# One core, two decoder layers: the convolution's taps, the last rows of the output projection and the prefetch depths are set anew

## The chip, the cores and the metric

The kernel runs on one core of a Trainium2 chip. The time is device microseconds of one launch. A core has TensorE (PE, matmuls), VectorE (DVE), ScalarE (ACT), GpSimd (POOL, hardly used here) and SyncE (SP, which issues the DMAs). Each works through its own queue of instructions in the order in which they stand; between queues there are only semaphores.

## The reference

Two layers on 256 tokens of 1024 features, in float32. A layer is a SwiGLU feed-forward part, a mixer, and a second feed-forward part; each reads an RMS norm of x and adds to x. The mixer is what the change touches:

```python
h = rms_norm(x, mix_norm[l])
p = h @ w_in[l]                                     # 19 tiles of 128 columns
a_val, a_gate, b_u, b_v, c_b, c_c, c_x = split(p)
a = a_val * sigmoid(a_gate)                         # group A: 384 channels
a = causal_depthwise_conv(a, conv_a_w[l]) + conv_a_b[l]      # 31 taps
a = silu(layer_norm(a, ln_a_g[l], ln_a_b[l]))
b = chunked_spatial_gating(gelu(b_u), gelu(b_v), ...)        # group B: 256 channels, a layer norm over v
c = c_b * causal_depthwise_conv(c_c * c_x, conv_c_w[l])      # group C: 384 channels, 3 taps
x = x + concatenate([a, b, c]) @ w_out[l]           # 8 blocks of 128 rows
```

## The kernel before, in words

**Weights.** All weights are one stream of pages of 128x1024 floats, in the order of their use. SyncE loads a page into one of RAWS buffers (`load_to`), ScalarE rounds it to a high part (`hi`, L157), and VectorE subtracts that from the page (`lo`, L158). The pairs lie in a pool of 30 buffers (`parts`, tag "pg"), which also holds the work tiles of the convolution. With a pair, a product of float32 numbers is three matmuls of the reduced type: high by high, high by low, low by high (`mm_three` L204 to L206, `mm_out` L216 to L218). `native` hands out the raw page instead, and `mm_out` then makes one float32 matmul (L212), which the trace shows as two records. `split_to` splits ahead of use as far as `state["cap"]` allows, `load_to` loads LOAD_AHEAD pages further.

**Mixer.** Layout is channels on partitions, tokens along the row. `proj` makes one of the 19 tiles of the combined projection, 24 matmuls of 128x256 each, 456 in all; their order is A (gate and value, three times), B's v and u, then for each of C's three tiles C_C, C_X, C_B. After each tile `drain(BACK)` issues four pieces of group A's convolution. `conv_ops` cuts the 31 taps of one 128-channel tile in two kinds: WIDE of them are products on ScalarE (L591, L594), four at a time into a 128x1024 tile, and VectorE adds each further four to the sum (L596); the rest are multiply-and-adds of 128x256 on VectorE (L603). L605 and L606 fold the four partial sums into the tile `m_ac`.

**Group B.** The layer norm over v takes a matmul for the mean (L565), squares, a matmul for the sum of squares (`m_lv_ps`, L336), the reciprocal root on VectorE as eleven small operations (L303 to L317, the last gives `m_lv_out`), and a broadcast on TensorE (`m_lv_pb`, L326). VectorE reads that (L723), then come transposes (`m_pt`, L732), copies, the gating matmuls (`m_pz`, L743), L749 and L756.

**Group C.** L690 to L703: `m_cc`, `zpad`, three taps, `m_cr`, and L703, which multiplies the C_B tile out of PSUM into the result (`m_co` or `m_cv`: buffers are used again, and names change). With the third tile only the three MM buffers of PSUM are left for projections (`use([MM], [SM])`), so the third C_B tile takes the buffer of the second, which L703 frees.

**Output projection (L764 on).** Rows of `w_out` come in OUT_ORDER (5, 6, 3, 4, 7, then group A's 0, 1, 2), four banks each. Between these matmuls stand the steps of group A's layer norm (`m_la`), after the matmuls whose counts CHAIN names. Then y (L781), Silu (L783), and the three rows of group A from native pages. `drain_banks` then finishes bank by bank, with the next norm's transposes (L393) between.

**Order.** Matmuls of the output projection and the sums are pinned to the order of the program; those of `proj` and everything on the other engines are put in order by the framework's scheduler, which works from costs of its own.

Of the kernel before, what the change touches and what calls it, by code (L numbers as in the profile page):

```python
# [20 lines left out]
DT = D // P  # L21
# [3 lines left out]
NA, NB, NC = 3, 2, 3  # L25
# [30 lines left out]
OUT_ORDER = (5, 6, 3, 4, 7, 0, 1, 2)  # L56

PAGE = 1024
RAWS = 6
PARTS = 15  # L60
LOAD_AHEAD = 6
AHEAD = 11
PACE = 1.6
NEXT = 4
WORK = 10
EVAC = 6
WARM = 8
LAG = 4
OPEN = 3
LAST = 3  # L70
CHAIN = (7, 11, 15)
STEPS = 3
AFTER = 2
WIDE = 16
BACK = 4


# [1 line left out]
def hybrid_trunk(ctx, tc, x_t, x_n, par, gain, w_st, b_s, wts, out):  # L79
    nc = tc.nc  # L80
    const = ctx.enter_context(tc.tile_pool(name="const", bufs=1))
    raws = ctx.enter_context(tc.tile_pool(name="raws", bufs=RAWS))
    parts = ctx.enter_context(tc.tile_pool(name="parts", bufs=2 * PARTS))
    acts = ctx.enter_context(tc.tile_pool(name="acts", bufs=1))
    work = ctx.enter_context(tc.tile_pool(name="work", bufs=WORK))
    tmp = ctx.enter_context(tc.tile_pool(name="tmp", bufs=2))
# [16 lines left out]
    banks = [(c, h) for h in range(2) for c in range(TC)]  # L103
    state = {"at": 0, "cap": None, "credit": 0.0, "mm": [], "sm": []}
# [3 lines left out]
    def use(mm, sm):  # L108

        state["mm"], state["sm"], state["outs"] = list(mm), list(sm), 0  # L110
# [14 lines left out]
    pages = []  # L125
# [3 lines left out]
    def after(ins, first):  # L129

        if first is not None:
            tc.add_manual_dep(
                ins.ins, first.ins.name,
                mybir.DependencyInfo(mybir.DependencyClass.NoSync, mybir.DependencyReason.DATA),
                reason="order",
            )
# [3 lines left out]
    def load_to(n):  # L140
        while len(loaded) < min(n, n_pages):
            i = len(loaded)
            raw = raws.tile([P, PAGE], F32, tag="raw", name=f"raw{i}")
            nc.sync.dma_start(raw, wts[i])
            loaded.append(raw)

    def split_to(n):

        while len(pages) < min(n, n_pages if state["cap"] is None else state["cap"]):
            i = len(pages)  # L150
            load_to(i + LOAD_AHEAD)
            hi = parts.tile([P, PAGE], F32R, tag="pg", name=f"hi{i}")
            lo = parts.tile([P, PAGE], F32R, tag="pg", name=f"lo{i}")
            step = PAGE if i > 3 else N
            for o in range(0, PAGE, step):
                cut = slice(o, o + step)
                nc.scalar.copy(hi[:, cut], loaded[i][:, cut])  # L157
                after(nc.vector.tensor_sub(lo[:, cut], loaded[i][:, cut], hi[:, cut]), held[0])  # L158
            pages.append((hi, lo))

    def native(n):

        at = state["at"]
        state["at"] += n
        load_to(at + n - 1 + LOAD_AHEAD)
        while len(pages) < at + n:
            pages.append(None)
        return loaded[at:at + n]

    def weights(n, ahead=True):  # L170

        at = state["at"]
        state["at"] += n
        last = at + n
        split_to(last)
        if ahead:
            state["credit"] += n * PACE
            to = min(last + AHEAD, len(pages) + int(state["credit"]))
            state["credit"] -= max(0, to - len(pages))
            state["credit"] = min(state["credit"], 2.0)  # L180
            split_to(to)
        return pages[at:at + n]
# [396 lines left out]
    def conv_ops(l, i, ap, out, name):  # L579
# [17 lines left out]

        single = list(range(WIDE, WA))
        groups = WIDE // 4
        for n in range(groups):  # L600
# [7 lines left out]
    def mixer(l, norm, nxt):  # L608
# [8 lines left out]
        use([MM, MM, MM, DD[0], DD[1]], [SM, DD[2], DD[3]])  # L617
        state["cap"] = state["at"] + NIN + OPEN

# [32 lines left out]
        def split_mix(k):  # L652
            if not halves:
                pair = parts.tile([P, 2, 2, T], F32R, tag="pg", name=f"{nm}_mix{k}")
                halves.extend([pair[:, 1], pair[:, 0]])
            x2 = halves.pop()
            nc.scalar.copy(x2[:, 0, :], mix[k])
            nc.vector.tensor_sub(x2[:, 1, :], mix[k], x2[:, 0, :])
            mix[k] = x2
# [106 lines left out]
        po = {b: ps_d.tile([P, N], F32, tag=f"d{b[0]}{b[1]}", name=f"{nm}_po{b[0]}{b[1]}")  # L766
              for b in banks}
        first, last = OUT_ORDER[0], OUT_ORDER[-1]
        state["cap"] = state["at"] + NB + NC
        ws = weights(NB + NC, False)  # L770
        ln = layer_norm(conv, LN_EPS, f"{nm}_la")
        got = None
        for n, k in enumerate(OUT_ORDER[:DT - NA]):
            for i, (c, h) in enumerate(banks):
                mm_out(po[c, h], mix[k], ws[n], c, h, k == first, k == last)
                if n * len(banks) + i in CHAIN:
                    got = next(ln)
        xc, pr = got
        for i in range(NA):
            y = single(f"{nm}_ay{i}")  # L780
# [1 line left out]
            a = single(f"{nm}_ao{i}")  # L782
            nc.scalar.activation(a, y, AF.Silu, scale=col(l, "ln_a_g", i), bias=col(l, "ln_a_b", i))  # L783
            mix[i] = a
        wn = dict(zip(OUT_ORDER[DT - NA:], native(NA)))
        state["cap"] = None
        split_to(state["at"] + NEXT)

# [88 lines left out]
```

## Time and profile before

| | us |
|---|---|
| median of 3 runs | 944.25 |
| lowest, highest | 943.35, 946.89 |
| profiled execution, time | 945.05 |
| profiled execution, span of the trace | 943.3 |
| PE busy in the span | 930.4 |
| DVE busy | 697.7 |
| ACT busy | 531.9 |

The span is cut by stages: feed-forward parts at 20 to 184, 292 to 464, 480 to 650 and 758 to 930 us, mixers at about 184 to 292 and 650 to 758 us. The trace's matmul records overlap: the length of one record is longer than the distance to the next, and the distance is what a matmul costs in a row of them. Where "x8" stands in a timeline row, eight equal instructions are drawn together, and the length is that of all. "[0.70 <-DVE m_co L703]" says that the engine sat idle for 0.70 us before and that VectorE's instruction of line 703 released it.

### The profile page before, as it was taken

Reading aid. Unit: us, or ns where it says so; the run is one execution under the profiler, and the core shown is the slowest. Engines: PE = TensorE matmul, PEld = TensorE weight load, DVE = VectorE, ACT = ScalarE, POOL = GpSimd, SP = SyncE. Lnnn points to the kernel's source line nnn. Section 1 sums busy time; section 2 is a strip of 40 time slices with the busy share of each in tenths; the row PEclk is TensorE's granted clock in tenths of the full one; section 3 lists DMA queues with packets and bytes.
Section 4 is the critical chain, followed back from the end, with each engine's and each line's share of the span. In section 5 each row is a group of like instructions: output and inputs, shape, how many; then the busy total and the mean of one; then the engine's idle time right before and its main releaser. Section 6 shows DMA issues by size and latency. Waiting matters only on the chain.

```text
span 943.3 us, 13962 instructions
## 1 busy us (share of the span) xinstructions
PE 930.4 (99%) x5192; PEld 799.7 (85%) x5192; DVE 697.7 (74%) x1195; ACT 531.9 (56%) x905; POOL 3.5 (0%) x14
## 2 busy tenths in 40 slices
PE   9999999999999999999999999999999999999996
PEld 8888888899868888888888888888998688888885
DVE  6996666589979976666697666666899798666624
ACT  5775454467457755545465545454755586555512
POOL 0000000000000000000000000000000000000000
PEclk9999999999999999999999999999999999999999
DMA  8897555524047955555465555553430588555201
GB/s 305 310 348 260 183 190 190 178 81 166 4 149 259 341 196 186 191 189 186 149 212 191 190 188 185 194 182 133 135 112 1 201 303 300 194 189 196 91 1 44
DMA packets 49459, 172.22 MB, mean 183 GB/s; under 512 B 5616, under 2 KB 7024, under 8 KB 49392
## 3 DMA queue, kind: packets, MB, share of 16 engines
q1 hardware_dynamic: 49392, 171.34, 51.6%
q8 instruction: 40, 0.66, 0.3%
q14 instruction: 27, 0.22, 0.1%
HBM read 170.27 MB, written 1.05 MB: 182 GB/s over the span
## 4 chain that ended last, share of the span: by engine, by line
PE 86%; DVE 9%; ACT 2%; issue 2%; DMA 1%; SPq 0%; DVEq 0%; ACTq 0%
PE f_pu L197 17%; PE f_pg L197 17%; PE f_pu L198 9%; PE f_pg L198 9%; PE f_pd L216 8%; PE f_pd L217 8%; PE f_pd L218 8%; DVE m_ac_acc L603 3%; DVE lo L158 2%; PE m_po L212 2%; DVE m_ac_acc L596 2%; PE m_p L204 1%; PE m_p L205 1%; PE m_p L206 1%; PE m_po L216 1%
## 5 line engine op out<-in xcount | busy, mean ns | idle before, releaser
L158 DVE TENSOR_TENSOR lo<-raw,hi 128x1024 fp32r<-128x1024 f32 (+1 forms) x310 | 376.0, 1218 | 166.1 <-ACT hi L157 147.0
L157 ACT CAST hi<-raw 128x1024 fp32r<-128x1024 f32 (+1 forms) x310 | 321.7, 1047 | 231.9 <-PE f_pu L197 79.6
L197 PE MATMUL f_pu<-ffn_norm_x,hi 128*128 128x512 f32 x696 | 250.1, 399 | 0.0
L197 PE MATMUL f_pg<-ffn_norm_x,hi 128*128 128x512 f32 x688 | 246.5, 398 | 0.0
L198 PE MATMUL f_pu<-ffn_norm_x,lo 128*128 128x256 f32 x696 | 195.2, 280 | 0.0
L198 PE MATMUL f_pg<-ffn_norm_x,lo 128*128 128x256 f32 x688 | 192.8, 280 | 0.0
L197 PEld LDWEIGHTS f_pu<-ffn_norm_x,hi 128*128 128x128 f32 x696 | 130.7, 188 | 31.9
L197 PEld LDWEIGHTS f_pg<-ffn_norm_x,hi 128*128 128x128 f32 x688 | 129.2, 188 | 31.0 <-issue 0.5
L216 PE MATMUL f_pd<-hi,f_m 128*128 128x512 f32 x352 | 138.7, 394 | 0.0
L217 PE MATMUL f_pd<-lo,f_m 128*128 128x512 f32 x352 | 137.8, 392 | 0.0
L218 PE MATMUL f_pd<-hi,f_m 128*128 128x512 f32 x352 | 137.2, 390 | 0.0
L198 PEld LDWEIGHTS f_pg<-ffn_norm_x,lo 128*128 128x128 f32 x688 | 129.7, 189 | 3.2 <-issue 0.5
L198 PEld LDWEIGHTS f_pu<-ffn_norm_x,lo 128*128 128x128 f32 x696 | 131.5, 189 | 0.1
L204 PE MATMUL m_p<-mix_norm_x,hi 128*128 128x256 f32 x304 | 87.2, 287 | 1.4 <-DVE m_co L703 0.7
L206 PE MATMUL m_p<-mix_norm_x,lo 128*128 128x256 f32 x304 | 86.0, 283 | 0.0
L205 PE MATMUL m_p<-mix_norm_x,hi 128*128 128x256 f32 x304 | 86.0, 283 | 0.0
L216 PEld LDWEIGHTS f_pd<-hi,f_m 128*128 128x128 f32 x352 | 66.1, 188 | 14.9
L218 PEld LDWEIGHTS f_pd<-hi,f_m 128*128 128x128 f32 x352 | 66.1, 188 | 14.4
L217 PEld LDWEIGHTS f_pd<-lo,f_m 128*128 128x128 f32 x352 | 66.1, 188 | 10.9
L204 PEld LDWEIGHTS m_p<-mix_norm_x,hi 128*128 128x128 f32 x304 | 58.3, 192 | 1.9 <-DVE m_co L703 0.9
L205 PEld LDWEIGHTS m_p<-mix_norm_x,hi 128*128 128x128 f32 x304 | 58.3, 192 | 0.1
L206 PEld LDWEIGHTS m_p<-mix_norm_x,lo 128*128 128x128 f32 x304 | 58.3, 192 | 0.0
(227 smaller groups left out, 820.8 us busy)
## 6 DMA issues: line engine op xcount, KB each, us to landing
raw<-wts SPq DMA_DIRECT2D x314, 512.0 KB, 4.3
xt<-x_t SPq DMA_DIRECT2D x4, 256.0 KB, 4.3
raw<-wts SPq DMA_DIRECT2D x8, 128.0 KB, 4.1
raw<-wts SPq DMA_DIRECT2D x4, 256.0 KB, 5.1
x_sb<-x_n SPq DMA_DIRECT2D x2, 512.0 KB, 6.6
out<-y SPq DMA_DIRECT2D x4, 256.0 KB, 2.2
wst<-w_st SPq DMA_DIRECT2D x2, 256.0 KB, 3.4
gfin<-gain SPq DMA_DIRECT2D x1, 512.0 KB, 4.3
```

Of the source, the lines that this page charges most:

```text
L157: nc.scalar.copy(hi[:, cut], loaded[i][:, cut])
L158: after(nc.vector.tensor_sub(lo[:, cut], loaded[i][:, cut], hi[:, cut]), held[0])
L197: pin(nc.tensor.matmul(ps, wh, x2, start=k == 0, stop=False))
L198: pin(nc.tensor.matmul(ps[:, 0, :], wl, x2[:, 0, :], start=False, stop=k == DT - 1))
L204: nc.tensor.matmul(ps, wh, x2[:, 0, :], start=k == 0, stop=False)
L205: nc.tensor.matmul(ps, wh, x2[:, 1, :], start=False, stop=False)
L206: nc.tensor.matmul(ps, wl, x2[:, 0, :], start=False, stop=k == DT - 1)
L212: put(nc.tensor.matmul(ps, x2[:, t], page[:, n], start=first, stop=last))
L216: put(nc.tensor.matmul(ps, xh, wh, start=first, stop=False))
L217: put(nc.tensor.matmul(ps, xh, wl, start=False, stop=False))
L218: put(nc.tensor.matmul(ps, xl, wh, start=False, stop=last))
L603: yield lambda j=j: nc.vector.scalar_tensor_tensor(acc[:, j % 4, :], ap[:, j:j + T], wt[j], acc[:, j % 4, :], ALU.mult, ALU.add)
```

## The change

WIDE goes from 16 to 24, so each convolution tile has six groups of four products on ScalarE instead of four and seven single taps on VectorE instead of fifteen. RAWS, LOAD_AHEAD and NEXT become one smaller, WORK (the buffers for single tiles) becomes 12, OPEN (pages that may be split ahead of the output projection) becomes 5, and CHAIN is earlier by one matmul group. In the output projection the three rows of group A are split in pairs (`split_mix`, as the other five are already) and their pages come from `weights` in place of `native`; three `split_to` calls stand among the matmuls. Lines behind the output projection's loop are four or five further down in the changed kernel: y is L784, Silu L786.

```diff
@@ -56,22 +56,22 @@
 OUT_ORDER = (5, 6, 3, 4, 7, 0, 1, 2)
 
 PAGE = 1024
-RAWS = 6
+RAWS = 5
 PARTS = 15
-LOAD_AHEAD = 6
+LOAD_AHEAD = 5
 AHEAD = 11
 PACE = 1.6
-NEXT = 4
-WORK = 10
+NEXT = 3
+WORK = 12
 EVAC = 6
 WARM = 8
 LAG = 4
-OPEN = 3
+OPEN = 5
 LAST = 3
-CHAIN = (7, 11, 15)
+CHAIN = (6, 10, 14)
 STEPS = 3
 AFTER = 2
-WIDE = 16
+WIDE = 24
 BACK = 4
 
 
@@ -766,15 +766,18 @@
         po = {b: ps_d.tile([P, N], F32, tag=f"d{b[0]}{b[1]}", name=f"{nm}_po{b[0]}{b[1]}")
               for b in banks}
         first, last = OUT_ORDER[0], OUT_ORDER[-1]
-        state["cap"] = state["at"] + NB + NC
+        state["cap"] = state["at"] + DT
         ws = weights(NB + NC, False)
         ln = layer_norm(conv, LN_EPS, f"{nm}_la")
         got = None
         for n, k in enumerate(OUT_ORDER[:DT - NA]):
             for i, (c, h) in enumerate(banks):
                 mm_out(po[c, h], mix[k], ws[n], c, h, k == first, k == last)
-                if n * len(banks) + i in CHAIN:
+                at = n * len(banks) + i
+                if at in CHAIN:
                     got = next(ln)
+                if at in (CHAIN[0] - 1, CHAIN[0], CHAIN[1]):
+                    split_to(len(pages) + 1)
         xc, pr = got
         for i in range(NA):
             y = single(f"{nm}_ay{i}")
@@ -782,7 +785,9 @@
             a = single(f"{nm}_ao{i}")
             nc.scalar.activation(a, y, AF.Silu, scale=col(l, "ln_a_g", i), bias=col(l, "ln_a_b", i))
             mix[i] = a
-        wn = dict(zip(OUT_ORDER[DT - NA:], native(NA)))
+        for i in range(NA):
+            split_mix(i)
+        wn = dict(zip(OUT_ORDER[DT - NA:], weights(NA, False)))
         state["cap"] = None
         split_to(state["at"] + NEXT)
```

The scheduler's order changes with it. VectorE, first layer, the stretch in which the reciprocal root of group B's norm is made (`m_lv_i` to `m_lv_out`; `m_ac_acc` is the third convolution tile's sum, `zpad` and `m_co` are group C's second tile). Before:

```order
L692 TENSOR_TENSOR zpad_132<-m_p_2693,m_cc_2727 128x256
L314 SCALAR_TENSOR_TENSOR m_lv_y<-m_lv_r,m_lv_i 128x2
L317 SCALAR_TENSOR_TENSOR m_lv_g<-m_lv_r,m_lv_g 128x2
L313 SCALAR_TENSOR_TENSOR m_lv_r<-m_lv_g,m_lv_y 128x2
L596 TENSOR_TENSOR m_ac_acc<-m_ac_acc,m_ac_t_2720 128x1024
L314 SCALAR_TENSOR_TENSOR m_lv_y<-m_lv_r,m_lv_y 128x2
L317 SCALAR_TENSOR_TENSOR m_lv_g<-m_lv_r,m_lv_g 128x2
L603 SCALAR_TENSOR_TENSOR m_ac_acc<-apad_130,par_sb,m_ac_acc 128x256
L313 SCALAR_TENSOR_TENSOR m_lv_r<-m_lv_g,m_lv_y 128x2
L698 SCALAR_TENSOR_TENSOR m_co_2_2629<-zpad_132,par_sb,m_co_2_2629 128x256
L314 SCALAR_TENSOR_TENSOR m_lv_out<-m_lv_r,m_lv_y 128x2
```

In the changed kernel the same steps stand like this:

```order
L314 SCALAR_TENSOR_TENSOR m_lv_y<-m_lv_r,m_lv_i 128x2
L317 SCALAR_TENSOR_TENSOR m_lv_g<-m_lv_r,m_lv_g 128x2
L596 TENSOR_TENSOR m_ac_acc<-m_ac_acc,m_ac_t_2712 128x1024
L313 SCALAR_TENSOR_TENSOR m_lv_r<-m_lv_g,m_lv_y 128x2
L698 SCALAR_TENSOR_TENSOR m_co_2_2682<-zpad_132,par_sb,m_co_2_2682 128x256
L603 SCALAR_TENSOR_TENSOR m_ac_acc<-apad_130,par_sb,m_ac_acc 128x256 x2
L314 SCALAR_TENSOR_TENSOR m_lv_y<-m_lv_r,m_lv_y 128x2
L317 SCALAR_TENSOR_TENSOR m_lv_g<-m_lv_r,m_lv_g 128x2
L605 TENSOR_TENSOR m_ac_acc<-m_ac_acc 128x512
L313 SCALAR_TENSOR_TENSOR m_lv_r<-m_lv_g,m_lv_y 128x2
L698 SCALAR_TENSOR_TENSOR m_co_2_2682<-zpad_132,par_sb,m_co_2_2682 128x256
L314 SCALAR_TENSOR_TENSOR m_lv_out<-m_lv_r,m_lv_y 128x2
```

Between the first of these small steps, L303, and `m_lv_out` stood one L596 before; now six L596, three L158, two L605, nine L603 and three L698 stand between them. L703 of group C's second tile follows `m_lv_out` three rows later, as the sixth before.

TensorE, first layer, the last projection tile (`m_p`, group C's third) and what follows the broadcast `m_lv_pb` (`m_pt` are group B's transposes, `m_po` the output projection). Before:

```order
L205 MATMUL m_p_2884<-mix_norm_x_1970,hi_2388 128x256
L206 MATMUL m_p_2884<-mix_norm_x_1970,lo_2389 128x256
L732 MATMUL m_pt_2811<-ident,m_bn_2_2777 128x128
L204 MATMUL m_p_2884<-mix_norm_x_1970,hi_2388 128x256
L205 MATMUL m_p_2884<-mix_norm_x_1970,hi_2388 128x256
L206 MATMUL m_p_2884<-mix_norm_x_1970,lo_2389 128x256
L732 MATMUL m_pt_2811<-ident,m_bn_2_2780 128x128
L216 MATMUL m_po_2917<-hi_2427,m_mix_2631 128x512
L217 MATMUL m_po_2917<-lo_2428,m_mix_2631 128x512
L218 MATMUL m_po_2917<-hi_2427,m_mix_2631 128x512
L732 MATMUL m_pt_2815<-ident,m_bn_2_2777 128x128
```

In the changed kernel:

```order
L205 MATMUL m_p_2909<-mix_norm_x_1967,hi_2399 128x256
L732 MATMUL m_pt_2845<-ident,m_bn_2_2815 128x128
L206 MATMUL m_p_2909<-mix_norm_x_1967,lo_2400 128x256
L204 MATMUL m_p_2909<-mix_norm_x_1967,hi_2399 128x256
L732 MATMUL m_pt_2845<-ident,m_bn_2_2818 128x128
L205 MATMUL m_p_2909<-mix_norm_x_1967,hi_2399 128x256
L206 MATMUL m_p_2909<-mix_norm_x_1967,lo_2400 128x256
L204 MATMUL m_p_2909<-mix_norm_x_1967,hi_2399 128x256
L205 MATMUL m_p_2909<-mix_norm_x_1967,hi_2399 128x256
L732 MATMUL m_pt_2849<-ident,m_bn_2_2815 128x128
L732 MATMUL m_pt_2849<-ident,m_bn_2_2818 128x128
```

The transposes stood behind 21 of the 24 matmuls of that tile and now stand behind 5, 7 and 11. `m_lv_pb` itself stands behind 432 of the 456 projection matmuls in both. `m_lv_ps` stood behind 336 of them in both layers and stands behind 346 in the first and 408 in the second layer.

ScalarE, first layer, output projection: Silu of group A's tiles (`m_ao`) with the load of its table. Before:

```order
L157 CAST hi_3055<-raw_2921 128x1024
L157 CAST hi_3061<-raw_2927 128x1024
L783 ACT_TABLE_LOAD
L783 ACTIVATE m_ao_2_3039<-m_la_q_2_2968,par_sb 128x256
L783 ACTIVATE m_ao_2_3042<-m_ao_2_3039,par_sb 128x256
L783 ACTIVATE m_ao_2_3045<-m_ao_2_3042,par_sb 128x256
L157 CAST hi_3067<-raw_3047 128x1024
L157 CAST hi_3073<-raw_3049 128x1024
```

In the changed kernel:

```order
L157 CAST hi_3032<-raw_2585 128x1024
L571 ACTIVATE m_la_q_2_2981<-m_la_q_2_2978 128x256
L786 ACT_TABLE_LOAD
L786 ACTIVATE m_ao_2_3067<-m_la_q_2_2981,par_sb 128x256
L786 ACTIVATE m_ao_2_3070<-m_ao_2_3067,par_sb 128x256
L786 ACTIVATE m_ao_2_3073<-m_ao_2_3070,par_sb 128x256
L657 CAST m_mix_2936<-m_ao_2_3067 128x256
L657 CAST m_mix_3077<-m_ao_2_3070 128x256
L657 CAST m_mix_3077<-m_ao_2_3073 128x256
L157 CAST hi_3084<-raw_2638 128x1024
```

The load of the table stood ahead of Silu's wait; in the changed kernel it waits for VectorE's y (L784) as the second layer's did before. Three rounding casts (`m_mix`, L657) now stand behind Silu, and VectorE's three subtractions (L658) for them behind y.

## Rows read from the trace of the kernel before

**Rows 1.** The page: span, and each engine's busy time, share of the span and instructions.

```profile
span 943.3 us, 13962 instructions
...
PE 930.4 (99%) x5192; PEld 799.7 (85%) x5192; DVE 697.7 (74%) x1195; ACT 531.9 (56%) x905; POOL 3.5 (0%) x14
```

**Rows 2.** Busy time of the engines by stretch: us, PE, PEld, DVE, ACT, POOL, PE's clock, DMA share, GB/s.

```profile
202.00:252.00 50.00, 49.30 (x409) 49.00 (x408) 46.95 (x100) 35.58 (x74) 0.00 (x0) 1.00 0.32 112
268.00:271.00 3.00, 3.00 (x8) 2.35 (x8) 2.24 (x9) 1.48 (x2) 0.00 (x0) 0.50 0.73 243
292.00:464.00 172.00, 172.00 (x911) 146.95 (x910) 126.41 (x185) 99.17 (x160) 0.00 (x0) 1.00 0.62 220
```

**Rows 3.** What TensorE waited for: line, releaser, us in all, times, longest.

```profile
PE m_la_ps L336 <- ACT m_la_q L571: 0.9, 1, 0.9
...
PE m_p L204 <- DVE m_co L703: 0.7, 1, 0.7
...
PE ffn_norm_pt L393 <- DVE x_sb L434: 0.5, 1, 0.5
```

**Rows 4.** TensorE's timeline, first layer's projection: start us, length us, operation, idle before.

```profile
236.32 0.95 PE L336 MATMUL m_lv_ps<-ones,m_lv_q 128*128 128x1 f32 x8
...
248.72 0.60 PE L326 MATMUL m_lv_pb<-ident,m_lv_out 128*128 128x128 f32 x4
250.03 0.39 PE L204 MATMUL m_p<-mix_norm_x,hi 128*128 128x256 f32 x1 [0.70 <-DVE m_co L703]
```

**Rows 5.** TensorE's timeline, second layer, projection and output projection.

```profile
701.52 0.95 PE L336 MATMUL m_lv_ps<-ones,m_lv_c 128*128 128x1 f32 x8
...
715.18 0.39 PE L204 MATMUL m_p<-mix_norm_x,hi 128*128 128x256 f32 x1 [0.66 <-DVE m_cv L703]
...
734.43 0.71 PE L326 MATMUL m_la_pb<-ident,m_la_out 128*128 128x128 f32 x4 [0.15 <-DVE m_la_out L314]
```

**Rows 6.** VectorE's timeline, first layer, around the last projection, and one split later.

```profile
246.56 0.15 DVE L314 SCALAR_TENSOR_TENSOR m_lv_y<-m_lv_r,m_lv_y 128x2 f32<-128x2 f32 x1
246.63 0.15 DVE L317 SCALAR_TENSOR_TENSOR m_lv_g<-m_lv_r,m_lv_g 128x2 f32<-128x2 f32 x1
...
249.56 0.41 DVE L703 TENSOR_TENSOR m_co<-m_p,m_cr 128x256 f32<-128x256 f32 x1
249.89 1.21 DVE L596 TENSOR_TENSOR m_ac_acc<-m_ac_acc,m_ac_t 128x1024 f32<-128x1024 f32 x1
251.02 0.41 DVE L658 TENSOR_TENSOR m_mix<-m_co,m_mix 128x256 fp32r<-128x256 f32 x1
...
256.51 0.47 DVE L603 SCALAR_TENSOR_TENSOR m_ac_acc<-apad,par_sb,m_ac_acc 128x256 f32<-128x256 f32 x1
256.90 0.42 DVE L756 TENSOR_TENSOR m_vt<-m_bz,m_bv 128x256 f32<-128x256 f32 x1
257.24 0.68 DVE L605 TENSOR_TENSOR m_ac_acc<-m_ac_acc 128x512 f32<-128x512 f32 x1
257.84 0.42 DVE L658 TENSOR_TENSOR m_mix<-m_vt,m_mix 128x256 fp32r<-128x256 f32 x1
...
734.29 1.22 DVE L158 TENSOR_TENSOR lo<-raw,hi 128x1024 fp32r<-128x1024 f32 x1
```

**Rows 7.** TensorE's timeline, first layer, output projection.

```profile
267.76 0.57 PE L218 MATMUL m_po<-hi,m_mix 128*128 128x512 f32 x1
...
271.63 0.61 PE L326 MATMUL m_la_pb<-ident,m_la_out 128*128 128x128 f32 x4
...
274.62 0.39 PE L218 MATMUL m_po<-hi,m_mix 128*128 128x512 f32 x1
274.85 4.45 PE L212 MATMUL m_po<-raw,m_ao 128*128 128x512 f32 x10
```

**Rows 8.** ScalarE's timeline, second layer, output projection.

```profile
735.93 1.28 ACT L783 ACT_TABLE_LOAD   x1
737.22 1.58 ACT L783 ACTIVATE m_ay<-m_ay,par_sb 128x256 f32<-128x256 f32 x3
```

## The prediction

> **What bounds the kernel now.** I read the busy times first: TensorE works 930.4 of 943.3 us [rows 1], and in a feed-forward stretch 172.00 of 172.00 us [rows 2]. So outside the two mixers nothing but TensorE's own work counts. In the mixer's projection it works 49.30 of 50 us, but VectorE works 46.95 and ScalarE only 35.58 [rows 2]: VectorE has 3.05 us to spare, ScalarE 14.4. The view of waits then says what little TensorE loses: 0.9 us in the first layer's output projection, 0.7 in each layer before the last projection tile, 0.5 at the second layer's transposes [rows 3]. The two timelines show where the 0.7 comes from: the last tile needs the PSUM buffer that L703 frees, and it starts at 250.03 and 715.18, 0.06 after L703's end in the first layer [rows 4 to 6]. VectorE's queue is thus already the last thing that TensorE waits for, and the question is what the change puts ahead of L703.
>
> **The change part by part.**
>
> *Taps.* In a layer 24 multiply-and-adds leave VectorE (0.39 us each, 9.4 us), six additions of 128x1024 come (1.13 each, start to start, 6.8 us) [rows 6]: 2.6 us less for VectorE. ScalarE gets 24 products; at the length of such an operation on VectorE, 0.47, that is 11 us of its 14.4 free, so it stays off the path. These counts alone would say: slightly better. The order says otherwise.
>
> *Where the queue waits.* `m_lv_ps` stands at a fixed place among TensorE's matmuls, and 409 records in 49.30 us make 0.12 us a matmul [rows 2]. First layer: it ends at 236.32 + 0.95 = 237.27 [rows 4], and ten matmuls more ahead of it make 238.5. VectorE cannot pass L303 before that. Behind L303, up to and with L703, there now stand nine operations of 128x1024 (six L596, three L158: 9 x 1.13 = 10.2; an L158 lasts 1.22, an L596 1.21), twelve multiply-and-adds (12 x 0.39 = 4.7), two L605 (2 x 0.60 = 1.2), nine others of 128x256 (9 x 0.34 = 3.1) and eleven small ones, between 0.07 (start to start) and 0.15 (length) each, 0.8 to 1.7, taken as 1.2 [rows 6]. That is 20.4 us, and L703 ends at 258.9 against 249.56 + 0.41 = 249.97: the last projection tile starts **8.9 us** later. TensorE has by then done everything ahead of it in order: `m_lv_pb` waits for nearly as long.
> Second layer: `m_lv_ps` ended at 701.52 + 0.95 = 702.47 [rows 5]; 72 matmuls more are 8.6 us, so 711.1. Behind L303 stand five of 128x1024 (5.65), ten multiply-and-adds (3.9), one L605 (0.6), nine of 128x256 (3.1) and the eleven small (1.2): 14.4, L703 at 725.5, the tile at 725.55 against 715.18: **10.4 us** later.
> What stands between that tile and group A's mean on TensorE is the same work less three matmuls, which move behind the mean, so the delay is carried through.
>
> *Pairs for group A's rows.* 24 records of L212 a layer, at 0.43 each when at full clock (ten take 4.45, the last one's tail of about 0.2 included) become 36 at 0.23 (274.62 to 274.85) [rows 7]: 10.3 against 8.3, **2.0 us less** in each layer.
>
> *Waits that go.* The 0.9 us in the first layer stood behind ScalarE's splits [rows 3]; with the convolution done by then, VectorE and ScalarE are idle ahead of the mean, and I take it as gone. After it TensorE ran slow: from 267.76 to 271.63 ten matmuls took 3.87 where ten at 0.23 take 2.3, 1.6 us more, at a granted clock of 0.50, which is 1.2 GHz of 2.4 [rows 2, 7]. That belongs to the wait and goes with it: **2.4 us** (0.87 + 1.57) in the first layer. In the second, 0.15 at `m_la_pb` [rows 5] and 0.5 at the transposes [rows 3]: **0.65 us**.
>
> *Waits that come.* The table load for Silu now stands behind y in both layers. In the second layer of before it did too: `m_la_pb` began at 734.43 and takes some 0.5, so TensorE went on at about 734.9; the load began at 735.93, three Silu end by 738.8 [rows 5, 8]. Now a cast of 0.41 (as any 128x256 move here [rows 6]) must follow before the first matmul of group A's rows can start, at 739.2. TensorE has 15 matmuls to do meanwhile (before: 12), 15 x 0.23 = 3.5, and is there at 738.4: **0.8 us** a layer. What queues behind ScalarE's wait are four splits for the next part; TensorE needs them only after group A's 36 matmuls, 8.3 us later.
> The other is what a gap of 9 us does to TensorE's clock, and the transposes that now stand among the last tile's matmuls, five matmuls (0.6 us) behind its start, where VectorE's two L723 (0.68) and a ScalarE step come first. Before shows both: no fall after the gap of 0.70 at 250.03 (the clock was 1.00 throughout 202 to 252 [rows 2]), and a fall costing 1.57 after the 0.9 one. The transposes wait some 0.8 us at full clock and nothing at half, so the two don't add. Between 0 and 1.6 I take **1.0 us** a layer, nearer to the second, as this gap is ten times as long.
> The Trainium skill (TensorE: Matmul & The Clock Gate, Part 1: The HAM clock gate) says that an idle array falls to 1.2 GHz and wins back 2.4 only by steady work. This trace agrees in one gap and not in the shorter one; by the rule the term would be 1.6 in each layer, by the 0.70 gap's row nothing.
> Of the table load the rows show 1.28 us and Silu at once behind it (735.93, 737.22) [rows 8]. The Trainium skill (ScalarE: Activation LUTs, What ACT_TABLE_LOAD costs) adds a drain of 1.38 us to each load; the trace shows none behind it. By the page Silu would be later by that, and the tail's wait 2.2 instead of 0.8; the sum goes by the row.
>
> *At nothing.* Five load buffers and one less ahead: feed-forward stretches run at TensorE's full 172.00 us with the DMA engines busy 0.62 [rows 2]; that cover stays unless a page lands late, and each late page would show at once. The twelve work tiles only loosen waits. NEXT is one split less ahead of matmuls that come 8.3 us later. OPEN puts two more splits, 2 x 1.13 us, on VectorE within the projection; they are counted above, in the L158 behind L303.
>
> *Sum.* First layer 8.9 - 2.0 - 2.4 + 0.8 + 1.0 = +6.3. Second 10.4 - 2.0 - 0.65 + 0.8 + 1.0 = +9.55. Together +15.85 on the profiled execution's 945.05, which is 960.9; that execution lay 0.8 above the median of its kernel's three runs, 944.25, so a median of **960 us**.
>
> **The rivals.**
> *VectorE is not held at L303* (0.12). If VectorE's slack covers part, only added work counts: what of the third convolution tile stood behind 249.97 before (two L596, eight L603, L605, L606: 2.3 + 3.1 + 0.6 + 0.3 = 6.3), less 2.6 for the taps, plus 2.3 for two splits, 6.0 us; less the 3.05 idle, 3.0. Between them 4.5 a layer: 4.5 - 2.0 - 2.4 + 0.8 + 0.5 = +1.4 and 4.5 - 2.0 - 0.65 + 0.8 + 0.5 = +3.15, 945.05 + 4.55 - 0.8 = 949. For it: 46.95 of 50 is a full queue, so little can wait. Against: L303 stands where it stands, and 20.4 us follow it.
> *The long queue costs nothing and the savings stay* (0.05). If TensorE's last tile is let in as before, because VectorE reaches L703 by 250, there remain -2.0 - 2.4 and -2.0 - 0.65, with 0.8 back in each: -5.45, 945.05 - 5.45 - 0.8 = 939. It decides if the 20.4 us behind L303 are under 11.5 (250.0 - 238.5); the durations of rows 6 would have to be wrong by nearly half.
> *ScalarE or the slow clock makes it worse* (0.09). If products come late from ScalarE, VectorE reaches L303 after 238.5; or the clock stays at half until group A's mean. About 24 matmuls at 0.12 and 21 at 0.23, 7.7 us, would then take twice as long, partly where TensorE waits anyway: some 4 us more in each layer than the 1.0 that I took gives, 968. Against: ScalarE keeps 3 of 50 us free even then.
>
> **How the numbers follow.** My forecast has 0.74, its own range is 954 to 966: 0.4 us either way for the small operations in each layer, 0 to 1.6 for the clock, 0 to 2.2 for the tail, and up to 2 us for operations that VectorE waits for inside the queue. With the first rival at 949 and the third at 968, 949 to 969 leaves out the rest. A measurement tells 0.5%, 4.7 us, from no change: 939.5 to 949.0 is "same". Faster 0.04 (the second rival's lower part), same 0.08 (the rest of it and the first rival's lower half), slower 0.88.
>
> **What would show it.** TensorE idle for 8 to 10 us in each layer just ahead of the last projection tile, at `m_lv_pb` or at its first L204, released by VectorE's `m_lv_out` or L703, at about 259 and 732 (the second shifted by the first layer's loss). VectorE without a gap from L303 to L703. No L212; group A's rows as L216 to L218 at 0.23 us, with a wait under 1 us ahead of the first. A granted clock under 1 right behind the gap. Feed-forward stretches as long as before. I am wrong if that idle time is under 4 us in either layer, if the gap stands somewhere else, or if a feed-forward part grows.

## The result, and the profile after

The changed kernel takes 971.9 us, the kernel before 943.8 on the same chips: a ratio of 1.0281 (95% interval 1.0265 to 1.0298), 28 us slower. One of its four executions took 5007 us; the ratio leaves it out, and the other three took 970.0 to 972.5. The forecast was 960, 16 us slower, with a range up to 969. The direction was right, and so was the place of the largest part of the loss; the loss is 12 us larger than the sum.

The page after, span and busy times:

```profile
span 970.8 us, 14046 instructions
...
PE 935.1 (96%) x5216; PEld 811.9 (84%) x5216; DVE 704.8 (73%) x1171; ACT 559.5 (58%) x965; POOL 3.2 (0%) x14
```

TensorE does 5 us more work than before by this count (slow matmuls are longer) and the span is 27.5 longer [rows 1]: the rest is idle time. The view of waits names it (line, releaser, us in all, times, longest):

```profile
PE m_lv_pb L326 <- DVE m_lv_out L314: 9.1, 2, 7.8
PE m_p L204 <- DVE m_cv L703: 7.3, 2, 6.5
PE ffn_norm_pt L393 <- DVE x_sb L434: 4.0, 2, 2.0
PE f_pg L197 <- DVE f_wu_sm L227: 2.7, 2, 1.6
PE m_p L204 <- DVE m_co L703: 1.8, 1, 1.8
```

The first, second and last of these stand where the gap was forecast, at the end of the projection; part of them stands one tile earlier, 1.8 in the first layer and 6.5 in the second. The transposes' wait (L393) was 0.5 [rows 3] and is 4.0, and the wait in the feed-forward part (f_pg on f_wu_sm) did not exist.

TensorE's timeline of the changed kernel, first layer, at the places that mark its course (start, length, operation, idle before):

```profile
238.09 0.72 PE L336 MATMUL m_lv_ps<-ones,m_lv_q 128*128 128x1 f32 x6
...
259.13 1.19 PE L326 MATMUL m_lv_pb<-ident,m_lv_out 128*128 128x128 f32 x4 [7.81 <-DVE m_lv_out L314]
260.24 0.58 PE L204 MATMUL m_p<-mix_norm_x,hi 128*128 128x256 f32 x1
...
271.85 1.46 PE L565 MATMUL m_la_mean<-m_ac,ones_sq 128*128 128x256 f32 x6
...
280.27 0.61 PE L326 MATMUL m_la_pb<-ident,m_la_out 128*128 128x128 f32 x4
...
290.35 0.66 PE L393 MATMUL ffn_norm_pt<-ident,x_sb 128*128 128x128 f32 x4 [2.01 <-DVE x_sb L434]
...
305.58 0.60 PE L326 MATMUL ffn_norm_pb<-ident,ffn_norm_out 128*128 128x128 f32 x4
```

And the second layer:

```profile
704.71 1.02 PE L565 MATMUL m_lv_mean<-m_bv,ones_sq 128*128 128x256 f32 x4
...
730.32 0.58 PE L204 MATMUL m_p<-mix_norm_x,hi 128*128 128x256 f32 x1 [6.50 <-DVE m_cv L703]
...
736.94 0.68 PE L326 MATMUL m_lv_pb<-ident,m_lv_out 128*128 128x128 f32 x4 [1.28 <-DVE m_lv_out L314]
738.47 0.39 PE L204 MATMUL m_p<-mix_norm_x,hi 128*128 128x256 f32 x1 [0.85 <-DVE m_cv L703]
...
749.81 0.59 PE L565 MATMUL m_la_mean<-m_ao,ones_sq 128*128 128x256 f32 x2
...
758.02 0.61 PE L326 MATMUL m_la_pb<-ident,m_la_out 128*128 128x128 f32 x4
...
783.40 0.60 PE L326 MATMUL ffn_norm_pb<-ident,ffn_norm_out 128*128 128x128 f32 x4
```

The rows of before at those marks that were not shown yet (the others are in [rows 4, 5, 7]):

```profile
260.58 1.46 PE L565 MATMUL m_la_mean<-m_ac,ones_sq 128*128 128x256 f32 x6
...
293.90 0.61 PE L326 MATMUL ffn_norm_pb<-ident,ffn_norm_out 128*128 128x128 f32 x4
...
692.02 1.02 PE L565 MATMUL m_lv_mean<-m_bv,ones_sq 128*128 128x256 f32 x4
...
725.71 0.59 PE L565 MATMUL m_la_mean<-m_ao,ones_sq 128*128 128x256 f32 x2
...
757.80 0.60 PE L326 MATMUL ffn_norm_pb<-ident,ffn_norm_out 128*128 128x128 f32 x4
```

Subtracting mark from mark gives the course of the loss. Last tile of the first layer: 260.24 against 250.03, +10.2. Group A's mean: +11.3. Its broadcast `m_la_pb`: 280.27 against 271.63, +8.6. Next norm's broadcast, behind the whole output projection: +11.7. Second layer's `m_lv_mean`: +12.7. Last tile: 738.47 against 715.18, +23.3. Mean: +24.1. `m_la_pb`: 758.02 against 734.43, +23.6. Norm's broadcast: +25.6. End of the span: +27.5. The marks at the mean and at `m_la_pb` stand behind three matmuls of the output projection fewer than before (CHAIN; 21 records of `m_po` in place of 24 from the last tile to the mean), 3 x 0.23 = 0.7 us, which come behind `m_la_pb` instead. At equal work the loss at these four marks is 0.7 larger. The loss rises in each projection, falls a little at group A's norm, as forecast, and rises again behind it, which was not.

VectorE's queue in the first layer, from L303 to the L703 that frees the last tile's buffer:

```profile
239.87 0.15 DVE L303 TENSOR_SCALAR m_lv_m<-m_lv_ps 128x2 f32<-128x2 f32 x1
...
259.76 0.42 DVE L703 TENSOR_TENSOR m_co<-m_p,m_cr 128x256 f32<-128x256 f32 x1
```

The work between takes 239.87 to 260.18, 20.3 us where the prediction had counted 20.4; only it began 1.4 later than 238.5: `m_lv_ps` ended 0.3 later (238.81), and VectorE, busy until then, was not there for another 1.1. No row of VectorE's from L303 to this L703 names a wait, so ScalarE's products were not late there. VectorE behind `m_la_pb` in the same layer:

```profile
284.63 1.10 DVE L658 TENSOR_TENSOR m_mix<-m_ao,m_mix 128x256 fp32r<-128x256 f32 x3 [2.63 <-ACT m_mix L657]
286.20 3.50 DVE L158 TENSOR_TENSOR lo<-raw,hi 128x1024 fp32r<-128x1024 f32 x3 [0.47 <-ACT hi L157]
289.61 0.68 DVE L434 TENSOR_TENSOR x_sb<-m_po,x_sb 128x512 f32<-128x512 f32 x1
```

Three splits (L158) stand between the subtractions for group A's rows (L658) and L434, which reads the first bank. They hold L434 until 289.61, and the transposes (290.35) wait 2.0 us for it. What the gaps do to the clock (stretch, us, PE, PEld, DVE, ACT, POOL, clock, DMA share, GB/s):

```profile
260.00:264.00 4.00, 4.00 (x19) 3.70 (x19) 1.27 (x4) 1.96 (x5) 0.00 (x0) 0.50 0.01 2
...
292.00:294.00 2.00, 2.00 (x6) 1.42 (x5) 1.11 (x2) 1.11 (x3) 0.00 (x0) 0.50 0.72 289
```

Behind the projection's gap TensorE runs at 0.50 for some four us, and again for two us behind the gap at the transposes.

### The profile page after: what moved, and what is told of

It reads as the page before. It is cut to its first block, busy times and chain, and to the rows that moved or that the text cites. A ratio compares the mean times of both kernels' runs of the same rounds, so it can differ in the third digit from the quotient of the medians.

```text
span 970.8 us, 14046 instructions
## 1 busy us (share of the span) xinstructions
PE 935.1 (96%) x5216; PEld 811.9 (84%) x5216; DVE 704.8 (73%) x1171; ACT 559.5 (58%) x965; POOL 3.2 (0%) x14
## 4 chain that ended last, share of the span: by engine, by line
PE 84%; DVE 9%; issue 2%; DMA 2%; ACT 2%; SPq 0%; DVEq 0%; ACTq 0%
PE f_pu L197 15%; PE f_pg L197 15%; PE f_pd L216 8%; PE f_pd L217 8%; PE f_pd L218 8%; PE f_pu L198 8%; PE f_pg L198 7%; PE m_p L204 3%; PE m_p L205 3%; PE m_p L206 3%; DVE lo L158 3%; DMA raw<-wts 2%; DVE m_ac_acc L596 1%; PE m_po L216 1%; ACT hi L157 1%
## 5 line engine op out<-in xcount | busy, mean ns | idle before, releaser
L158 DVE TENSOR_TENSOR lo<-raw,hi 128x1024 fp32r<-128x1024 f32 (+1 forms) x316 | 383.1, 1219 | 164.4 <-ACT hi L157 145.1
L157 ACT CAST hi<-raw 128x1024 fp32r<-128x1024 f32 (+1 forms) x316 | 329.3, 1047 | 236.8 <-PE f_pg L197 79.5
L217 PE MATMUL f_pd<-lo,f_m 128*128 128x512 f32 x352 | 137.9, 392 | 0.0
L204 PE MATMUL m_p<-mix_norm_x,hi 128*128 128x256 f32 x304 | 89.8, 295 | 9.2 <-DVE m_cv L703 7.3
L206 PE MATMUL m_p<-mix_norm_x,lo 128*128 128x256 f32 x304 | 88.9, 292 | 0.0
L205 PE MATMUL m_p<-mix_norm_x,hi 128*128 128x256 f32 x304 | 88.5, 291 | 0.0
L217 PEld LDWEIGHTS f_pd<-lo,f_m 128*128 128x128 f32 x352 | 66.1, 188 | 10.9
L204 PEld LDWEIGHTS m_p<-mix_norm_x,hi 128*128 128x128 f32 x304 | 60.5, 199 | 10.4 <-DVE m_cv L703 7.6
L205 PEld LDWEIGHTS m_p<-mix_norm_x,hi 128*128 128x128 f32 x304 | 60.6, 199 | 0.3 <-issue 0.2
L206 PEld LDWEIGHTS m_p<-mix_norm_x,lo 128*128 128x128 f32 x304 | 60.6, 200 | 0.2 <-issue 0.2
```

Source lines behind the costliest of these rows:

```text
L204: nc.tensor.matmul(ps, wh, x2[:, 0, :], start=k == 0, stop=False)
L205: nc.tensor.matmul(ps, wh, x2[:, 1, :], start=False, stop=False)
L206: nc.tensor.matmul(ps, wl, x2[:, 0, :], start=False, stop=k == DT - 1)
L217: put(nc.tensor.matmul(ps, xh, wl, start=False, stop=False))
```

## The experiments

Ratios are to the kernel before, run on the same chip. All are against 943.8 to 945.6 us.

**Taps back to 16 in the changed kernel.**

```diff
-WIDE = 24
+WIDE = 16
```

> The changed kernel with the taps alone undone (WIDE 16). Theory Q (VectorE's queue ahead of L703 makes the gap before the last projection tile): in the order of this kernel only 4.6 us of VectorE's work lie between L303 and m_lv_out, as before the change, so the gaps of 7.8 and 1.8 us in the first layer and 6.5, 1.3 and 0.9 in the second shrink to about 0.7 each and the half-clock stretch behind them goes; 971.9 - about 21 = 950 to 952. Theory T (the loss sits at the end of the output projection, where VectorE's splits stand ahead of the first bank's read): this kernel keeps that, so 4.0 us of waits at the transposes (L393) stay. Rival R (five load buffers and two more early splits load VectorE): within 3 us of 971.9.

Measured 952.7 us, ratio 1.0084 (1.0066 to 1.0101). Its waits:

```profile
PE ffn_norm_pt L393 <- DVE x_sb L434: 3.6, 2, 2.0
PE m_lv_pb L326 <- DVE m_lv_out L314: 2.5, 2, 1.3
```

The gaps of the projection are gone but for 1.3 at `m_lv_pb` and 1.5 at the last tile in each layer; the transposes' wait stays at 3.6. The taps are shown to be worth 19 of the 28 us, as theory Q has it; of the 7.9 that stay, 3.6 are the wait of theory T.

**Splits behind the banks in the changed kernel.**

```diff
-        split_to(state["at"] + NEXT)
-
         def bank(c, h, between=None):
+            n = banks.index((c, h))
+            split_to(state["at"] + (NEXT if n == 3 else n))
```

> The changed kernel with the NEXT splits for the feed-forward part issued one by one behind each bank instead of all ahead of the first. Theory T: one L158 instead of three stands between the last L658 and L434; the wait of 2.0 us at L393 goes in each layer and with it the half-speed stretch behind it of about 2 us: 971.9 - 8 = 964, a little less gain if the feed-forward part then waits more for splits than the 2.7 us it waits now. Rival: the wait moves to the first matmuls of the feed-forward part, 970 or more. The gaps in the projection stay as they are by every theory.

Measured 965.1 us, ratio 1.0214 (1.0197 to 1.0231), 6.8 us less than the changed kernel.

```profile
PE m_lv_pb L326 <- DVE m_lv_out L314: 7.5, 2, 6.3
...
PE ffn_norm_pt L393 <- DVE x_sb L434: 0.7, 2, 0.4
```

The wait at L393 falls from 4.0 to 0.7, the gaps of the projection stay. From `m_la_pb` to the next norm's broadcast, in both layers:

```profile
280.45 0.61 PE L326 MATMUL m_la_pb<-ident,m_la_out 128*128 128x128 f32 x4
...
302.60 0.61 PE L326 MATMUL ffn_norm_pb<-ident,ffn_norm_out 128*128 128x128 f32 x4
...
755.21 0.61 PE L326 MATMUL m_la_pb<-ident,m_la_out 128*128 128x128 f32 x4
...
777.38 0.61 PE L326 MATMUL ffn_norm_pb<-ident,ffn_norm_out 128*128 128x128 f32 x4
```

That is 22.2 us in each, where the changed kernel takes 25.3 and 25.4: 6.4 of the 6.8 us. The splits ahead of L434 are shown to be the cause of the loss there.

**24 taps alone in the kernel before** (WIDE 24).

> The kernel before with the taps alone changed (WIDE 24). Theory Q: behind L303 stand 18.1 us of VectorE's work up to the L703 that frees the last tile's buffer in the first layer, 13.0 in the second, and m_lv_ps stands 8 to 10 and 61 to 63 matmuls later: last tile 6.6 and 7.8 us late, 1 us of clock each, less 2.5 for the waits in the output projection that go: about 957. Rival (24 taps are free on an engine with 14 us to spare, only the other edits hurt): 944 or below.

Measured 961.0 us, ratio 1.0172 (1.0157 to 1.0188): 16 us of the loss with one number changed, more than the 13 expected, and far from the rival's none.

**Pairs alone in the kernel before** (the edits of the output projection and CHAIN; every other number as before).

> The kernel before with group A's rows in pairs alone (CHAIN, cap and the three early splits with them; 16 taps, 6 load buffers, NEXT 4, OPEN 3, WORK 10 as before). Prediction's term: 2.0 us less in each layer and 0.8 back, about 941 to 942. Theory T: four L158 behind the three L658 stand ahead of L434, one more than in the changed kernel, so a wait of 2 to 3 us at L393 and a half-speed stretch of 2 in each layer: 949 to 954, and the wait named there is L393 on x_sb.

Measured 953.5 us, ratio 1.0093 (1.0078 to 1.0108). The edit by itself loses, where the prediction's term is a gain.

```profile
PE ffn_norm_pt L393 <- DVE x_sb L434: 5.7, 2, 3.1
PE m_la_ps L336 <- ACT m_la_q L571: 1.5, 2, 0.9
PE m_po L217 <- DVE lo L158: 1.4, 1, 1.4
```

Besides the transposes (5.7), the sums of squares wait for splits on ScalarE in both layers, and 1.4 us go to a split that comes too late in the output projection. That OPEN 3, with eight rows that now need a pair, makes it late is likely and was not tested by itself.

**Three pieces after each projection tile** in the changed kernel: the same work in another order.

```diff
-BACK = 4
+BACK = 3
```

> The changed kernel with three pieces of the convolution issued after each projection tile instead of four (BACK 3): the same work on every engine, in another order. Theory Q: m_lv_ps is back behind 336 projection matmuls, and behind L303 stand 17.1 and 17.5 us of VectorE's work up to the L703 that frees the last tile's buffer (before the change 6.8, with the change 20.4 and 14.4 behind a later m_lv_ps). L303 can run at 237.3, so that L703 ends at about 254.4 in place of 260.2: 5 to 6 us less in each layer, about 960. Rival S (ScalarE's 24 products come too late, whatever the order): no gain, 970 or more.

Measured 963.6 us, ratio 1.0200 (1.0179 to 1.0222); 8 us less than the changed kernel, where 11 to 12 were expected.

```profile
PE m_p L204 <- DVE m_co L703: 5.7, 1, 5.7
PE m_pt L732 <- ACT m_by L725: 5.1, 1, 5.1
```

The first layer's tile starts at 255.38, one us behind the 254.4 of Q. In the second layer the wait moved into the tile, to group B's transposes (5.1). ScalarE has the same 24 products and the time changes with the order, so rival S falls for this kernel.

**Two pieces, in the kernel before with 24 taps** (WIDE 24, BACK 2).

> The kernel before with 24 taps on ScalarE and two pieces after each projection tile (BACK 2). In its order only 3.7 us of VectorE's work stand between L303 and m_lv_out and 8.2 up to L703 of the second C tile, as before the change 4.6 and 6.8; but the third convolution tile's last pieces come behind the projection. Theory Q: no gap ahead of the last projection tile, so the 24 taps cost nothing there; either group A's mean then waits for the third tile (up to 5 us a layer, 950), or VectorE's lighter load shows as 0.7 less in each layer: 942 to 944. Rival S: 957 or more, as with 24 taps and four pieces (961.0).

Measured 969.5 us, ratio 1.0255 (1.0239 to 1.0271): a miss in size. Half of what was expected came true, no gap ahead of the last tile; but

```profile
PE m_la_mean L565 <- DVE m_ac L606: 23.3, 2, 12.1
```

the mean of group A's norm waits 12.1 and 11.3 us for the third tile's `m_ac`, not up to 5. What leaves the queue ahead of L703 comes back behind it. The time lies in the range of rival S, and here products do come late: ScalarE makes twenty of the third tile's from 258.66 to 266.75, behind the projection, and VectorE works on their sums until 273.5. The pieces were issued later; how much of the wait is ScalarE's and how much VectorE's was not separated.

**Group A's mean one group earlier in the kernel before** (CHAIN 6, 11, 15).

> The kernel before with CHAIN (6, 11, 15): group A's mean one group of matmuls earlier, the sum of squares still after the same one, so five groups lie between them. The wait of 0.87 at m_la_ps in the first layer and the half-speed stretch behind it (1.57) should go: 944.8 - 2.4 = 942.4. Rival (the fall of the clock comes from the twelve one-column matmuls, not from the wait): the wait goes, the half-speed stretch stays, 944.

Measured 946.3 us, ratio 1.0009 (0.9999 to 1.0019): no change. Both theories had it wrong: the wait stays, probably since ScalarE's splits move with the squares, and a split is late elsewhere.

```profile
PE m_po L217 <- DVE lo L158: 1.2, 1, 1.2
...
PE m_la_ps L336 <- ACT m_la_q L571: 0.9, 1, 0.9
```

But TensorE's clock did not fall behind that same wait in this execution (0.50 from 268 to 271 in the kernel before [rows 2]):

```profile
268.00:270.00 2.00, 2.00 (x10) 1.66 (x9) 1.83 (x9) 0.49 (x1) 0.00 (x0) 1.00 0.85 270
```

**Six load buffers in the changed kernel** (RAWS and LOAD_AHEAD 6).

> The changed kernel with six load buffers and six loads ahead (RAWS, LOAD_AHEAD 6). Open is the wait of f_pg on f_wu_sm in the feed-forward part behind each mixer, 1.1 and 1.6 us, that the kernel before doesn't have and the kernel with pairs alone (six buffers, NEXT 4) doesn't either. Theory L (five buffers make pages late there): it goes, 969. Theory N (NEXT 3 and late splits make it): it stays, 971 to 972.

Measured 968.0 us, ratio 1.0238 (1.0221 to 1.0256). The wait on f_wu_sm is gone from the view: theory L. Five buffers cost 3.9 us. Behind the two mixers ScalarE's splits wait for pages to land, 4.3 us (from 286 to 330) and 5.6 us (from 750 to 830) in the changed kernel, 1.8 and 0.5 here.

**Three causes undone in the changed kernel** (WIDE 16, splits behind the banks, six buffers).

> The changed kernel with 16 taps, the NEXT splits one by one behind the banks, and six load buffers: the three causes named so far undone, the pairs, CHAIN, OPEN 5, NEXT 3 and twelve work tiles kept. If the three account for the loss: 952.7 (16 taps alone) - 3.6 (waits at L393) - 1.7 (waits on f_wu_sm) = 947 to 948, of which 2 us are the two more early splits on VectorE (gaps of 1.3 and 1.5 ahead of the last tile in place of 0.7), so the rest stands within 2 us of the kernel before. If something else of the change costs time: 950 or more.

Measured 949.1 us, ratio 1.0051 (1.0036 to 1.0066). That is 23 of 28 us, and between the two expectations; what is left, 4.6, went to the run on OPEN below.

**A faster kernel with pairs?** (16 taps, pairs, splits behind the banks, OPEN 4, CHAIN as in the changed kernel, the other numbers as before.)

> An attempt at a faster kernel: 16 taps, pairs for group A's rows, splits behind the banks, six load buffers, NEXT 4, OPEN 4, ten work tiles. Behind L303 stand 7.6 us of VectorE's work up to L703 (6.8 before). The prediction's own term for the pairs, 2.0 us less in each layer, should now show, less 1 us for the cast behind Silu and 0 to 1 for waits at m_la_ps: 942 to 946. Rival: with one early split less than in the changed kernel the first splits of the output projection come late as with the pairs alone (1.4 us at L217): 947.

Measured 952.5 us, ratio 1.0082 (1.0066 to 1.0097): neither expectation.

```profile
PE ffn_norm_pt L393 <- DVE x_sb L434: 3.0, 2, 1.5
PE m_p L204 <- DVE m_co L703: 2.2, 1, 2.2
...
PE ffn_norm_pb L326 <- DVE ffn_norm_out L314: 2.1, 2, 1.0
```

With NEXT 4 the fourth bank has two splits ahead of its read (L393 and the norm's broadcast wait 1.5 and 1.0 in each layer), and the 7.6 us of work up to L703 came with a gap of 2.2.

**The additions on GpSimd**, in the changed kernel with late splits, six buffers and NEXT 4:

```diff
-                nc.vector.tensor_add(acc, acc, t)
+                nc.gpsimd.tensor_add(acc, acc, t)
```

> The changed kernel with the fifteen additions of 128x1024 of each layer's convolution (L596) on GpSimd, which does nothing in the mixer, and with late splits, six load buffers and NEXT 4. 17 us of each layer's work leave VectorE. Theory Q: behind L303 stand 11.0 and 9.8 us up to the L703 that frees the last tile's buffer, so it ends at about 250 in the first layer, as before the change, and no gap over 1 us is left: 942 to 948, if an addition on GpSimd takes under about 3 us (45 us for fifteen). If GpSimd takes longer, or slows VectorE, group A's mean waits for m_ac: 955 or more.

Measured 995.2 us, ratio 1.0538 (1.0522 to 1.0553). An addition takes 2.4 us there (min, median, max in ns):

```profile
L596 POOL TENSOR_TENSOR m_ac_acc<-m_ac_acc,m_ac_t x30: 2337/2412/4171, 209.8 to 760.1; 128x1024 f32<-128x1024 f32 x30
```

That is under the 3 us allowed, and still the kernel is far slower. The condition was wrong: the partial sums are one chain through both engines, and VectorE waits in order. Who waited for these sums (us, times), among others:

```profile
  DVE m_ac_acc L603: 34.4, 16
```

VectorE's multiply-and-adds waited 34.4 us for GpSimd's additions; where VectorE makes both, the same view lists no such wait.

**The same in the kernel before.**

> The kernel before with its nine additions of 128x1024 of each layer (L596) on GpSimd and nothing else changed. Theory Q: 10 us of each layer's work leave VectorE, behind L303 stand 5.7 us up to L703, the 0.7 us ahead of the last tile go, and m_la_ps waits as before: 943 to 945. If GpSimd's additions are slow (over 4 us) or slow VectorE: 948 or more, with m_la_mean waiting for m_ac.

Measured 968.8 us, ratio 1.0254 (1.0239 to 1.0271), a miss for the same reason (its multiply-and-adds waited 17.7 us for GpSimd's additions), with TensorE's wait at the other place:

```profile
PE m_lv_pb L326 <- DVE m_lv_out L314: 20.7, 2, 10.5
```

**Only the two overlooked terms undone** (24 taps kept; splits behind the banks, six buffers).

> The changed kernel with 24 taps kept and only the two terms undone that the prediction did not have: the NEXT splits one by one behind the banks, and six load buffers. If these two are what the prediction missed, the time falls by the 6.8 us of the first and the 3.9 us of the second, 971.9 - 10.7 = 961, which is the prediction's own sum (960). If the prediction's projection or pair terms were wrong too and balanced by chance, it need not: 955 or 967.

Measured 962.7 us, ratio 1.0191 (1.0173 to 1.0209), within 2 of the expectation and 3 of the forecast.

```profile
PE m_lv_pb L326 <- DVE m_lv_out L314: 9.0, 2, 7.8
...
PE ffn_norm_pt L393 <- DVE x_sb L434: 0.7, 2, 0.4
```

The projection's gaps are all there, the other two waits are gone or down to 0.7. From `m_la_pb` to the next norm's broadcast this kernel takes 22.2 us in each layer, as with the splits behind the banks alone; the kernel before takes 22.3 and 23.4, with three matmuls (0.7 us) less to do there. Part of the closeness to the forecast is luck: in its second layer TensorE was back at full clock ahead of the last tile, and the stretch from there to the mean cost only 0.3 at equal work, where it cost 1.5 in the changed kernel.

**OPEN 5 alone in the kernel before.**

> The kernel before with OPEN 5 alone: two more pages are split during the projection, 2.3 us of VectorE's work ahead of L303 (39.8 in place of 37.5). Theory Q: the gap ahead of the last tile grows by up to 2.3 us in each layer, less what m_la_ps then no longer waits for splits: 944.5 + 2 to 4 = 946 to 948. That is what stays in the kernel with the three causes undone (949.1). Rival (the two splits are hidden): 944.5 or, without the wait at m_la_ps, 942.

Measured 947.9 us, ratio 1.0041 (1.0026 to 1.0056): 2.8 us, inside the 2 to 4 of theory Q. The row of `m_lv_pb` is the same as in the changed kernel with 16 taps (2.5, 2, 1.3), and so are the two gaps of 1.5 at the last tile: they belong to the two early splits. What TensorE's clock does behind these gaps differs. First the kernel with three causes undone, then this one, first layer, from 252 to 262 us:

```profile
252.00:262.00 10.00, 9.91 (x59) 8.30 (x60) 8.78 (x20) 2.65 (x6) 0.00 (x0) 0.83 0.01 2
...
252.00:262.00 10.00, 9.64 (x65) 7.75 (x66) 9.93 (x23) 3.03 (x7) 0.00 (x0) 1.00 0.07 11
```

The last tile starts at 252.09 and 252.36 behind the same gaps (1.28 and 1.48); in one kernel the clock falls, in the other it doesn't. From that tile to the mean the first takes 1.5 us longer at equal work, and the same in the second layer.

**Sums of squares one group later in the kernel before** (CHAIN 7, 12, 15).

> An attempt at a faster kernel: the kernel before with CHAIN (7, 12, 15), the sums of squares one group of matmuls later (0.92 us), so that the wait of 0.87 at m_la_ps in the first layer has matmuls in it. Expected: that wait and the half-speed stretch behind it gone, 942 to 943; the broadcast then waits up to 0.9 us in the second layer, where m_la_out was late by 0.15 already. Rival: what is won at m_la_ps is lost at m_la_pb, 944 to 945.

Measured 945.9 us, ratio 1.0012 (1.0001 to 1.0023). The wait at m_la_ps is gone, and up to 0.8 us in each layer stand instead at a matmul of the output projection that waits for a split (L217 on L158): the rival, if at another place. No kernel of this study beats the kernel before.

## Why the prediction was wrong, step by step

*Where the queue waits: right.* The mechanism and its price were read from the order and the rows of before: 8.9 and 10.4 us were forecast, 10.2 and 10.6 (23.3 less the 12.7 before it) measured. The 1.3 in the first layer is the late start at L303. That the order and not ScalarE's load decides is shown by BACK alone, and by VectorE's stretch without a wait. The place was right in part: 1.8 us in the first layer and 6.5 in the second stand ahead of the last tile but one, and only 2.1 of the second layer's gap are at the last tile. Two of the prediction's own signs of being wrong came true, this one and a feed-forward part that grows.

*What the gap does to the clock: the fall was right, its size too small.* 1.0 a layer was put. From the last tile to the mean the loss grows by 1.1 and 0.8 with three matmuls less in the stretch, so by 1.8 and 1.5 at equal work, nearer to the 1.6 that the prediction named as its upper end.

*Waits that go: right for the norm.* 2.4 and 0.15 at the sums and the broadcast, measured 2.6 and 0.5. The 0.5 at the second layer's transposes did not go; it grew (next step).

*Waits that come: the step that failed.* The prediction said of the splits behind Silu: "TensorE needs them only after group A's 36 matmuls, 8.3 us later". That is true of the splits and overlooks VectorE's queue: their second halves (L158) stand ahead of L434, and the next norm's transposes wait for that one. From `m_la_pb` to the next norm's broadcast the forecast was -2.0 + 0.8, and 0.5 less in the second layer; with the 0.7 us of matmuls that moved here, -0.5 and -1.0 us. It was +3.0 and +2.0. Splitting behind the banks (second experiment) brought it to -0.1 and -1.2: 6.4 of the 6.5 us too much are this queue. Of these, 3.3 are the waits at L393, and much of the rest is the clock, which now stays at 1.00 where it had fallen to 0.50, from 292 to 294 and from 770 to 772.

*At nothing, five load buffers: wrong.* The cover was read from feed-forward stretches of the kernel before. In the changed kernel pages land late behind the mixers, and 1.0 and 1.9 us are lost in the feed-forward parts. With six buffers put back ScalarE waits less for pages, these parts are as short as before, and the kernel gains 3.9 us.

*Pairs: right once the tail's queue is out of the way.* 2.0 us a layer were to be won on TensorE; less the tail's 0.8, and with the 0.5 of the second layer, 1.2 and 1.7. With the two terms above undone the stretch takes 22.2 us in each layer against 22.3 and 23.4; with 0.7 us more work in it, that is 0.8 and 1.9 won at equal work. What the term left out is that a pair is bought with a split (L158) and a subtraction (L658) on VectorE for each row. With OPEN 5 a part of that lies in the projection, where VectorE is the engine waited for, and OPEN 5 alone costs 2.8 us. No kernel with pairs was faster than the kernel before.

The 12 us between forecast and result add up, first and second layer: 1.3 and 0.2 (the last tile's start), 0.8 and 0.5 (clock), 3.5 and 3.0 (tails), 1.0 and 1.9 (feed-forward parts), less 0.2 and 0.4 (more waits gone at the norm than forecast). With the tail and the buffers undone the kernel comes out at 962.7 where the prediction had 960.

The Trainium skill's rule that an idle array falls to 1.2 GHz (TensorE: Matmul & The Clock Gate, Part 1: The HAM clock gate) agrees with the trace behind each long gap, 0.50 from 260 to 264. The clock also fell behind gaps of 2.0 us at the transposes, and behind 1.3 and 1.5 in one kernel and not in another. The drain that the Trainium skill adds to a table load (ScalarE: Activation LUTs, What ACT_TABLE_LOAD costs) did not show: in the first layer Silu starts at 282.71, at the end of the load (281.42 + 1.28), and group A's first matmul waited 0.3 us in each layer, not 2.2.

The kernel with three causes undone (949.1) is 1.2 above OPEN 5 alone. Its trace has 1.5 us more a layer from the last tile to the mean, behind the clock's fall, and waits of 0.7 at `m_la_ps` and 1.4 at `m_la_pb`, against what the pairs win. Open is why the clock falls behind a wait of 0.87, or gaps of 1.3 and 1.5, in one kernel and not in another; each was profiled once, so it may differ between executions of one kernel too.

## What to carry to other kernels

Price an added wait by the queue of the engine that waits, not only by the data that comes late: list everything that stands behind the waiting instruction on that engine, and who needs each. Where a scheduler orders the queues, a change in the number of pieces can move whole chains; the count of work between two named instructions, times durations of the trace, gave the start of the last tile to within 2 us in the changed kernel. The count alone failed where the work between waits for another engine, as with two pieces and with GpSimd. When marks of two kernels are subtracted, check that the same work stands between them. A trade of matmul time for vector work is judged by the engine that is waited for in that stage, however idle it looks in the total.

## What the runs showed of the hardware

TensorE's clock fell to 0.50 behind a wait of 0.87 us with one-column matmuls on both sides in the kernel before [rows 2, 3], and stayed at 1.00 behind the same wait in the kernel with CHAIN 6, 11, 15. Behind the same two gaps of 1.28 and 1.48 us its mean from 252 to 262 was 0.83 in one kernel and 1.00 in another. An addition of 128x1024 floats takes 2.4 us on GpSimd and 1.2 on VectorE, and VectorE's multiply-and-adds were hardly slower beside it (478 ns, against 474 in the kernel before).
